# Rotary embedding on one core: float32 instead of bf16, two hardware DMA queues, products split over VectorE and GpSimd

## Chip, core and metric

The kernel runs on one core of a Trainium2 chip. The metric is device time in microseconds (us). The span is the time from the first to the last instruction in the profile; single executions run about 1.7 us above it (170.15 us against 168.4 us before the change). Runs marked slow (over 1.5% above the fastest of the same kernel) are left out of the ratios.

## The reference

x has shape (8, 2048, 8, 64) in float32: batch, position, head, dimension. cos and sin are (2048, 32).

```python
x1, x2 = x[..., :32], x[..., 32:]
out1 = x1 * cos - x2 * sin          # cos, sin broadcast over batch and head
out2 = x1 * sin + x2 * cos
out  = concatenate([out1, out2], axis=-1)
```

x and the output are 33.55 MB each, and the two tables 0.26 MB each. That is 67.6 MB to move for four products and two sums per pair of elements.

## The kernel before

Each of the 128 partitions holds 16 consecutive positions of one batch; a tile is 4 of them, 2048 elements a partition. There are 32 tiles. Everything on chip is bf16. All DMA is issued on GpSimd's queue, and the DMA casts between float32 in DRAM and bf16 in SBUF, the on-chip memory. VectorE does all arithmetic.

```python
for t in range(num_tiles):                       # 32 loads, 20 buffers
    xt = xpool.tile([P, FREE], bf16, tag="xt", name=f"xt{t}")
    nc.gpsimd.dma_start(out=..., in_=xv[b, :, l*SL:(l+1)*SL, :])
...
for t in range(num_tiles):
    eng.tensor_mul(out=t1k, in0=xtv, in1=cb)     # eng is nc.vector
    eng.tensor_mul(out=t2k, in0=xtv, in1=sb)
    eng.tensor_sub(out=otv[:, :, 0:Dh], in0=t1v[:, :, 0:Dh], in1=t2v[:, :, Dh:D])
    eng.tensor_add(out=otv[:, :, Dh:D], in0=t2v[:, :, 0:Dh], in1=t1v[:, :, Dh:D])
    nc.gpsimd.dma_start(out=ov[...], in_=ot...)  # 12 output buffers
```

## Time and profile before

| | before |
|---|---|
| time, median (range) | 170.2 us (169.31 to 170.33), 4 runs |
| span of the profiled run | 168.4 us |
| VectorE busy | 111.7 us, 66% |
| GpSimd busy | 35.3 us, nearly all of it issuing DMA |
| DMA | at nine tenths or more in slices 1 to 37 of 0 to 39 |

The first lines are from the page of the kernel before: busy tenths per slice (40 equal slices of 4.2 us), what the DMA moved per slice, and the HBM totals. DVE is VectorE and POOL is GpSimd.

```profile
DVE  0059999999999950000008999999999999960000
POOL 7512212211221221222122122212212111120000
DMA  3999999999999999999999999999999999999970
GB/s 53 158 209 214 212 214 214 210 215 215 212 214 212 214 212 214 215 213 212 231 414 422 432 426 430 426 428 428 430 426 426 430 428 428 428 426 430 430 267 2
...
HBM read 34.08 MB, written 33.55 MB: 402 GB/s over the span
```

The DMA row is the one without gaps. The step in the GB/s row from about 214 to about 428 is no change of speed. The first half is loads, which are counted as the bf16 bytes they land; each of those bytes is two bytes read. All 67.6 MB at 428 GB/s take 158 us.

Next, groups of instructions: line, engine, operation, output<-inputs, shapes, count | busy us in total, mean ns of one | idle time before them and what ended it.

```profile
L91 DVE TENSOR_TENSOR t<-xt,cos_sb 128x2048 bf16<-128x2048 bf16 x32 | 38.9, 1216 | 10.6 <-DMA xt<-in_x_dram 10.4
...
L98 DVE TENSOR_TENSOR ot<-t,t 128x1024 bf16<-128x1024 bf16 x32 | 21.8, 682 | 27.7 <-DMA out_dram<-ot 27.7
...
L101 POOL DMA_DIRECT2D out_dram<-ot x32 | 17.0, 532 | 65.9 <-DMA out_dram<-ot 29.1 <-DVE ot L99 21.6 <-DMA xt<-in_x_dram 15.2
```

And the waits (who waited for whom: total us, times, longest):

```profile
DVE ot L98 <- DMA out_dram<-ot: 27.7, 1, 27.7
...
DVE t L91 <- DMA xt<-in_x_dram: 10.4, 1, 10.4
```

VectorE waited once for 27.7 us because all output buffers were full and their stores stood behind the loads in one queue. It is an engine with time to spare. The bytes set the time.

### The profile page before, as it was taken

Reading aid. Unit: us, or ns where it says so; the run is one execution under the profiler, and the core shown is the slowest. Engines: PE = TensorE matmul, PEld = TensorE weight load, DVE = VectorE, ACT = ScalarE, POOL = GpSimd, SP = SyncE. Lnnn points to the kernel's source line nnn. Section 1 sums busy time; section 2 is a strip of 40 time slices with the busy share of each in tenths; the row PEclk is TensorE's granted clock in tenths of the full one; section 3 lists DMA queues with packets and bytes.
Section 4 is the critical chain, followed back from the end, with each engine's and each line's share of the span. In section 5 each row is a group of like instructions: output and inputs, shape, how many; then the busy total and the mean of one; then the engine's idle time right before and its main releaser. Section 6 shows DMA issues by size and latency. Waiting matters only on the chain.

```text
span 168.4 us, 282 instructions
## 1 busy us (share of the span) xinstructions
DVE 111.7 (66%) x128; POOL 35.3 (21%) x70
## 2 busy tenths in 40 slices
DVE  0059999999999950000008999999999999960000
POOL 7512212211221221222122122212212111120000
DMA  3999999999999999999999999999999999999970
GB/s 53 158 209 214 212 214 214 210 215 215 212 214 212 214 212 214 215 213 212 231 414 422 432 426 430 426 428 428 430 426 426 430 428 428 428 426 430 430 267 2
DMA packets 9506, 50.61 MB, mean 300 GB/s; under 512 B 1056, under 2 KB 1312, under 8 KB 5408
## 3 DMA queue, kind: packets, MB, share of 16 engines
q0 software_dynamic: 9504, 50.60, 103.5%
q14 instruction: 2, 0.02, 0.0%
HBM read 34.08 MB, written 33.55 MB: 402 GB/s over the span
## 4 chain that ended last, share of the span: by engine, by line
DMA 51%; DVE 24%; issue 12%; POOL 2%; POOLq 0%; DVEq 0%; PEldq 0%
DMA xt<-in_x_dram 39%; DMA out_dram<-ot 12%; DVE t L91 8%; DVE t L92 6%; DVE ot L98 5%; DVE ot L99 5%; POOL out_dram L101 2%; POOL cos_sb L44 0%; POOLq L130 0%; POOL sin_sb L45 0%; POOLq L101 0%; DVEq L98 0%; PEldq L130 0%; POOLq L70 0%
## 5 line engine op out<-in xcount | busy, mean ns | idle before, releaser
L91 DVE TENSOR_TENSOR t<-xt,cos_sb 128x2048 bf16<-128x2048 bf16 x32 | 38.9, 1216 | 10.6 <-DMA xt<-in_x_dram 10.4
L98 DVE TENSOR_TENSOR ot<-t,t 128x1024 bf16<-128x1024 bf16 x32 | 21.8, 682 | 27.7 <-DMA out_dram<-ot 27.7
L92 DVE TENSOR_TENSOR t<-xt,sin_sb 128x2048 bf16<-128x2048 bf16 x32 | 38.9, 1216 | 0.0
L101 POOL DMA_DIRECT2D out_dram<-ot x32 | 17.0, 532 | 65.9 <-DMA out_dram<-ot 29.1
L70 POOL DMA_DIRECT2D xt<-in_x_dram x32 | 16.9, 541 | 48.6 <-DMA xt<-in_x_dram 44.7
L99 DVE TENSOR_TENSOR ot<-t,t 128x1024 bf16<-128x1024 bf16 x32 | 21.8, 681 | 0.0
L44 POOL DMA_DIRECT2D cos_sb<-in_cos_dram x1 | 0.7, 667 | 0.8 <-PEq L130 0.8
L45 POOL DMA_DIRECT2D sin_sb<-in_sin_dram x1 | 0.5, 543 | 0.0
L119 POOL MEMSET const-float32-0.0<- 128x1 f32 x1 | 0.1, 98 | 0.2 <-issue 0.2
L119 POOL MEMSET const-bfloat16-1.0<- 128x1 bf16 x1 | 0.1, 101 | 0.0
L119 POOL MEMSET const-float32-1.0<- 128x1 f32 x1 | 0.1, 98 | 0.0
L119 POOL MEMSET const-uint8-127<- 128x1 uint8 x1 | 0.1, 98 | 0.0
## 6 DMA issues: line engine op xcount, KB each, us to landing
out_dram<-ot POOLq DMA_DIRECT2D x32, 1024.0 KB, 19.1
xt<-in_x_dram POOLq DMA_DIRECT2D x32, 512.0 KB, 19.1
cos_sb<-in_cos_dram POOLq DMA_DIRECT2D x1, 128.0 KB, 3.2
sin_sb<-in_sin_dram POOLq DMA_DIRECT2D x1, 128.0 KB, 3.1
```

The lines of the kernel that those rows point to most:

```text
L44: nc.gpsimd.dma_start(out=cos_sb, in_=cos_src)
L45: nc.gpsimd.dma_start(out=sin_sb, in_=sin_src)
L70: nc.gpsimd.dma_start(out=xt.rearrange("p (r f) -> p r f", r=SL), in_=xv[b, :, l * SL : (l + 1) * SL, :],)
L91: eng.tensor_mul(out=t1k, in0=xtv, in1=cb)
L92: eng.tensor_mul(out=t2k, in0=xtv, in1=sb)
L98: eng.tensor_sub(out=otv[:, :, 0:Dh], in0=t1v[:, :, 0:Dh], in1=t2v[:, :, Dh:D])
L99: eng.tensor_add(out=otv[:, :, Dh:D], in0=t2v[:, :, 0:Dh], in1=t1v[:, :, Dh:D])
L101: nc.gpsimd.dma_start(out=ov[b, :, l * SL : (l + 1) * SL, :], in_=ot.rearrange("p (r f) -> p r f", r=SL),)
L119: nc = _bacc.Bacc("TRN2", target_bir_lowering=False, num_devices=1)
```

## The change

The intent is to compute in float32 throughout without paying for it. The DMA no longer casts, and it moves to the queues of the sync engine (loads) and the scalar engine (stores). GpSimd is then free to do half of the products. Each VectorE product and add in the tile loop reads one operand from PSUM, a second on-chip memory, so that it has only one input in SBUF. The tiles also come in another order (batch innermost). The diff, cut to its core:

```diff
-    nc.gpsimd.dma_start(out=cos_sb, in_=cos_src)          # bf16 tables
-    nc.gpsimd.dma_start(out=sin_sb, in_=sin_src)
+    nc.scalar.dma_start(out=sin_sb, in_=sin_src)          # float32 tables
+    nc.scalar.dma_start(out=cos_sb, in_=cos_src)
...
-        xt = xpool.tile([P, FREE], bf16, ...); nc.gpsimd.dma_start(out=xt..., ...)
+        xt = xpool.tile([P, FREE], f32, ...);  nc.sync.dma_start(out=xt, ...)
...
+    nc.vector.tensor_scalar_mul(ssin[:, :, 0, :], sin_sb, -1.0)   # signed sin
+    nc.vector.tensor_copy(ssin[:, :, 1, :], sin_sb)
+    nc.vector.tensor_copy(cos_ps, cos_sb)                         # cos to PSUM
...
-        eng.tensor_mul(out=t1k, in0=xtv, in1=cb)
-        eng.tensor_mul(out=t2k, in0=xtv, in1=sb)
-        eng.tensor_sub(...); eng.tensor_add(...)
-        nc.gpsimd.dma_start(out=ov[...], in_=ot...)
+        for u in range(2):                                # halves swapped
+            nc.gpsimd.tensor_mul(out=dst..., in0=src..., in1=rep(ssin[..., u, :], H))  # t2, SBUF, 3 buffers
+        nc.vector.tensor_mul(out=t1..., in0=xt..., in1=rep(cos_ps[...], 2 * H))         # t1, PSUM, 1 buffer
+        nc.vector.tensor_add(out=xt, in0=t1, in1=t2)      # in place
+        nc.scalar.dma_start(out=ov[...], in_=xt)
```

More of the change, by code (lines that the diff above doesn't have):

```diff
@@ L20 @@
     f32 = mybir.dt.float32
-    bf16 = mybir.dt.bfloat16
     B, S, H, D = x.shape
@@ L31 @@
     FREE = SL * HD
-    NH = SL * H
-    NK = NH * 2
-    xv = x.rearrange("b (q r) h d -> b q r (h d)", q=P)
-    ov = out.rearrange("b (q r) h d -> b q r (h d)", q=P)
+    xv = x.rearrange("b (q r) h d -> b q (r h d)", q=P)
+    ov = out.rearrange("b (q r) h d -> b q (r h d)", q=P)
     cos_src = cos.rearrange("(q r) d -> q r d", q=P)
@@ L41 @@
     const_pool = ctx.enter_context(tc.tile_pool(name="const", bufs=1))
-    cos_sb = const_pool.tile([P, R, Dh], bf16, tag="cb")
-    sin_sb = const_pool.tile([P, R, Dh], bf16, tag="sb")
-    nc.gpsimd.dma_start(out=cos_sb, in_=cos_src)
-    nc.gpsimd.dma_start(out=sin_sb, in_=sin_src)
-    num_tiles = B * n_blk
-    xpool = ctx.enter_context(tc.tile_pool(name="xpool", bufs=20))
-    tpool = ctx.enter_context(tc.tile_pool(name="tpool", bufs=4))
-    opool = ctx.enter_context(tc.tile_pool(name="opool", bufs=12))
@@ L53, in coef @@
-    def coef(tab, l):
-        a = tab[:, l * SL, :]
-        return dataclasses.replace(
-            a, ap=[a.ap[0][:], [Dh, SL], [0, 2 * H], a.ap[1][:]]
-        )
-    def idx(t):
-        b = t // n_blk
-        l = t % n_blk
-        return b, l
-    eng = nc.vector
-    xts = []
-    for t in range(num_tiles):
-        b, l = idx(t)
-        xt = xpool.tile([P, FREE], bf16, tag="xt", name=f"xt{t}")
-        nc.gpsimd.dma_start(
-            out=xt.rearrange("p (r f) -> p r f", r=SL),
-            in_=xv[b, :, l * SL : (l + 1) * SL, :],
-        )
-        xts.append(xt)
@@ L76 @@
-    for t in range(num_tiles):
-        b, l = idx(t)
-        xt = xts[t]
-        t1 = tpool.tile([P, FREE], bf16, tag="t1")
-        t2 = tpool.tile([P, FREE], bf16, tag="t2")
-        ot = opool.tile([P, FREE], bf16, tag="ot")
-        cb = coef(cos_sb, l)
-        sb = coef(sin_sb, l)
-        xtv = xt.rearrange("p (r k d) -> p r k d", r=SL, d=Dh)
-        t1k = t1.rearrange("p (r k d) -> p r k d", r=SL, d=Dh)
-        t2k = t2.rearrange("p (r k d) -> p r k d", r=SL, d=Dh)
-        eng.tensor_mul(out=t1k, in0=xtv, in1=cb)
-        eng.tensor_mul(out=t2k, in0=xtv, in1=sb)
-        t1v = t1.rearrange("p (h d) -> p h d", d=D)
-        t2v = t2.rearrange("p (h d) -> p h d", d=D)
-        otv = ot.rearrange("p (h d) -> p h d", d=D)
-        eng.tensor_sub(out=otv[:, :, 0:Dh], in0=t1v[:, :, 0:Dh], in1=t2v[:, :, Dh:D])
-        eng.tensor_add(out=otv[:, :, Dh:D], in0=t2v[:, :, 0:Dh], in1=t1v[:, :, Dh:D])
-        nc.gpsimd.dma_start(
-            out=ov[b, :, l * SL : (l + 1) * SL, :],
-            in_=ot.rearrange("p (r f) -> p r f", r=SL),
-        )
+    cps_pool = ctx.enter_context(tc.tile_pool(name="cps", bufs=1, space=bass.MemoryType.PSUM))
@@ new lines @@
+    t1_pool = ctx.enter_context(tc.tile_pool(name="t1p", bufs=1, space=bass.MemoryType.PSUM))
+    xpool = ctx.enter_context(tc.tile_pool(name="xpool", bufs=20))
+    t2_pool = ctx.enter_context(tc.tile_pool(name="t2p", bufs=3))
+    cos_sb = const_pool.tile([P, R, Dh], f32, tag="cb")
+    sin_sb = const_pool.tile([P, R, Dh], f32, tag="sb")
+    ssin = const_pool.tile([P, R, 2, Dh], f32, tag="ss")
+    cos_ps = cps_pool.tile([P, R, Dh], f32, tag="cp")
+    nc.scalar.dma_start(out=sin_sb, in_=sin_src)
@@ new lines, with rep @@
+    nc.scalar.dma_start(out=cos_sb, in_=cos_src)
+    tiles = [(b, l) for l in range(n_blk) for b in range(B)]
+    xts = []
+    for i, (b, l) in enumerate(tiles):
+        xt = xpool.tile([P, FREE], f32, tag="xt", name=f"xt{i}")
+        nc.sync.dma_start(out=xt, in_=xv[b, :, l * FREE : (l + 1) * FREE])
+        xts.append(xt)
+    nc.vector.tensor_scalar_mul(ssin[:, :, 0, :], sin_sb, -1.0)
+    nc.vector.tensor_copy(ssin[:, :, 1, :], sin_sb)
+    nc.vector.tensor_copy(cos_ps, cos_sb)
+    def rep(a, n):
+        return dataclasses.replace(a, ap=[a.ap[0][:], a.ap[1][:], [0, n], a.ap[-1][:]])
@@ new lines @@
+    for i, (b, l) in enumerate(tiles):
+        xt = xts[i]
+        t1 = t1_pool.tile([P, FREE], f32, tag="t1")
+        t2 = t2_pool.tile([P, FREE], f32, tag="t2")
+        for u in range(2):
+            dst = t2.rearrange("p (rh u d) -> p rh u d", u=2, d=Dh)[:, :, u, :]
+            src = xt.rearrange("p (rh u d) -> p rh u d", u=2, d=Dh)[:, :, 1 - u, :]
+            nc.gpsimd.tensor_mul(
+                out=dst.rearrange("p (r h) d -> p r h d", h=H),
+                in0=src.rearrange("p (r h) d -> p r h d", h=H),
+                in1=rep(ssin[:, l * SL : (l + 1) * SL, u, :], H),
+            )
+        nc.vector.tensor_mul(
+            out=t1.rearrange("p (r k d) -> p r k d", r=SL, d=Dh),
+            in0=xt.rearrange("p (r k d) -> p r k d", r=SL, d=Dh),
+            in1=rep(cos_ps[:, l * SL : (l + 1) * SL, :], 2 * H),
+        )
+        nc.vector.tensor_add(out=xt, in0=t1, in1=t2)
+        nc.scalar.dma_start(out=ov[b, :, l * FREE : (l + 1) * FREE], in_=xt)
```

## The prediction

> **What bounds the kernel now.** The DMA engines. In the page's 40 slices DMA is at nine tenths or more from slice 1 to slice 37. The slices before 78 us move about 214 GB/s, those after about 428 GB/s. These are one rate: in the first half the transfers are loads that write bf16, so each byte landed is two bytes read from HBM. Totals agree: 34.08 MB read and 33.55 MB written; 67.6 MB at 428 GB/s is 158 us. Stretch by stretch, DMA starts at about 2.4 us and dies away at 164 us; 4.2 us follow with no transfer. VectorE is 66% busy (bf16 products 1216 ns, half-tile sub and add 682 ns). Its longest waits, in the waits view, are for DMA: 27.7 us once for an output buffer, 10.4 us for the first tile. So VectorE has slack and bytes set the time.
>
> **What the change does.** HBM bytes stay the same: x and out were float32 in DRAM already; only the cast inside the DMA goes. So the roughly 158 us of transfer stays. Removed: 64 issues of 0.53 us on GpSimd, which were not the bound. Added: GpSimd arithmetic. Loads and stores now have separate queues, so they mix instead of running as a load half and a store half.
>
> VectorE: the bf16 records fit (n/2+143) cycles at 0.96 GHz. At one float32 element per cycle a 2048-element op is (2048+143)/0.96 = 2.28 us. Two a tile plus PSUM effects: about 4.6 us, 32 tiles 147 us.
>
> GpSimd: this trace has no arithmetic of it. The Trainium skill, "GPSIMD Engine Reference", section 3.1, gives 4497 ns for a float32 2048-element tensor_tensor (VectorE 2293 ns). Estimate from it: two 1024-element halves take 4.5 to 4.7 us a tile, 32 tiles 147 us. No run here shows it yet.
>
> Contention: the skill's "SBUF — State Buffer", section "Who interferes with whom", says that a VectorE instruction with at most one SBUF input, outside two-port modes, doesn't contend with GpSimd. Here product and add each read one operand from PSUM, so I expect both engines to run at full rate side by side.
>
> **Critical path after.** Two bounds nearly meet.
> Compute: first tile and sin table usable near 7 us, 64 GpSimd ops at 2.33 us start to start end at 156 us, last add 2.3, last store 4.5, end of program 2.2: span 165 us.
> Transfer: start 2 us, 67.6 MB at 415 to 428 GB/s (mixing reads and writes may cost a little) 158 to 163 us, end 4.2: span 164 to 169 us.
> The larger decides; times run 1.7 us above the span (170.15 against 168.4). I predict 168.5 us, 80% range 163.5 to 178. Chances: faster by over 2% 0.28, within 2% 0.45, slower by over 2% 0.27. Doubling VectorE's work per tile costs little as it had slack; the gain is small as the bytes stay.
>
> **What would show each step.**
> - GpSimd: 64 products of about 2.3 us each, 85 to 90% busy from 7 to 156 us.
> - VectorE: 64 ops of about 2.3 us, near 147 us busy; waits short, for t2.
> - DMA slices flat near 415 to 428 GB/s with loads and stores mixed; two queues in place of one; mean near 400 GB/s over the span. No half-rate first half.
> - First VectorE tile op near 6 to 7 us instead of 10.4 us.
> - The chain that ended last alternates GpSimd products and adds, or DMA waits for xt, near the end one store.
>
> **What would make it wrong.** GpSimd slower than estimated with 32-element strided runs: each 0.1 us per op adds 6.4 us. VectorE and GpSimd contending after all: serial, over 200 us. Mixed traffic well under 415 GB/s: 400 would give 177 us. Or mixing faster than 428 GB/s and GpSimd faster than estimated: down to 160 us.

## The result and the profile after

| | before | after |
|---|---|---|
| time, median (range) | 170.2 us (169.31 to 170.33) | 168.09 us (168.06 to 168.34) |
| span of the profiled run | 168.4 us | 166.6 us |
| VectorE busy | 111.7 us | 148.2 us |
| GpSimd busy | 35.3 us (DMA issue) | 146.3 us (products) |

The ratio is 0.9887, with a 95% interval of 0.986 to 0.9914: 1.1% faster, which is "within 2%" in the prediction's terms. Ratios here are the mean time of one kernel's fast runs over that of the other's in the same rounds, so they are not quite the ratio of the medians. The output is correct.

The same lines of the page of the kernel after:

```profile
DVE  0169999999999999999999999999999999999980
POOL 0299999999999999999999999999999999998000
DMA  5999999999999999999999999999999999999656
GB/s 167 424 428 421 374 431 423 433 427 425 431 421 431 429 427 427 425 433 419 433 425 423 433 419 433 423 433 427 425 431 421 431 427 427 429 423 433 285 220 252
...
HBM read 34.08 MB, written 33.55 MB: 406 GB/s over the span
```

The transfer rate is about 427 GB/s from slice 1 to slice 36 (slice 4 apart), and loads and stores now run mixed. The new thing is at the right end: the DMA row falls to 6, 5, 6 while the DVE row still shows 9 and 8. At the end the transfers wait for VectorE, where before VectorE was long done. The groups:

```profile
L73 POOL TENSOR_TENSOR t<-xt,ssin 128x1024 f32<-128x1024 f32 x64 | 146.1, 2341 | 6.8 <-DVE ssin L58 6.8
L78 DVE TENSOR_TENSOR t<-xt,cos_ps 128x2048 f32<-128x2048 f32 x32 | 73.5, 2296 | 1.1
L83 DVE TENSOR_TENSOR xt<-t,t 128x2048 f32<-128x2048 f32 x32 | 73.3, 2291 | 3.3
L60 DVE COPY cos_ps<-cos_sb 128x512 f32<-128x512 f32 x1 | 0.7, 694 | 2.4 <-DMA cos_sb<-in_cos_dram 2.4
```

A VectorE instruction takes 2.29 us for 2048 float32 elements. GpSimd's 64 products fill 146.1 us, which is 2.283 us from start to start; the mean of 2341 ns is larger because records overlap. Now the chain of work that ended last, in order of time (start us, length us, what):

```profile
1.17 8.72 DMA cos_sb<-in_cos_dram
...
9.91 0.70 DVE cos_ps L60
...
10.64 2.31 DVE t L78
...
13.04 2.30 DVE xt L83
...
15.37 2.31 DVE t L78
...
159.52 2.29 DVE xt L83
```

The chain starts with the DMA that brings the cos table: issued at 1.17 us, landed at 9.89. From 10.64 on it is VectorE alone, product and add in turn. The last add starts at 159.52 us and takes 2.29. From the first product to the end of the last add is 151.2 us, or 4.725 us a tile: 4.587 us of work and about 0.14 us between instructions. The page's line puts shares to it:

```profile
DVE t L78 44%; DVE xt L83 44%; DMA cos_sb<-in_cos_dram 5%; DVE cos_ps L60 0%; DVEq L83 0%; ACTq L48 0%
```

Finally stretches of time (start:end, length, busy us of VectorE and GpSimd with counts, clock, DMA share, GB/s):

```profile
160.00:162.00 2.00, 1.81 (x1) 0.00 (x0) 1.00 0.17 70
162.00:164.00 2.00, 0.00 (x0) 0.00 (x0) 1.00 0.73 303
```

Between 160 and 162 us the DMA engines are 17% busy, with the end of the store before the last. Then they have nothing left but the last tile, which VectorE hands over at 161.8 us.

### The profile page after: what moved, and what is told of

The parts are those of the page before. It is cut to its first block, busy times and chain, and to the rows that moved or that the text cites. A ratio compares the mean times of both kernels' runs of the same rounds, so it can differ in the third digit from the quotient of the medians.

```text
span 166.6 us, 381 instructions
## 1 busy us (share of the span) xinstructions
DVE 148.2 (89%) x67; POOL 146.3 (88%) x68
## 3 DMA queue, kind: packets, MB, share of 16 engines
q10 hardware_dynamic: 4896, 34.08, 48.6%
HBM read 34.08 MB, written 33.55 MB: 406 GB/s over the span
## 4 chain that ended last, share of the span: by engine, by line
DVE 89%; DMA 5%; issue 2%; DVEq 0%; ACTq 0%
DVE t L78 44%; DVE xt L83 44%; DMA cos_sb<-in_cos_dram 5%; DVE cos_ps L60 0%; DVEq L83 0%; ACTq L48 0%
## 5 line engine op out<-in xcount | busy, mean ns | idle before, releaser
L73 POOL TENSOR_TENSOR t<-xt,ssin 128x1024 f32<-128x1024 f32 x64 | 146.1, 2341 | 6.8 <-DVE ssin L58 6.8
L83 DVE TENSOR_TENSOR xt<-t,t 128x2048 f32<-128x2048 f32 x32 | 73.3, 2291 | 3.3
L78 DVE TENSOR_TENSOR t<-xt,cos_ps 128x2048 f32<-128x2048 f32 x32 | 73.5, 2296 | 1.1
L60 DVE COPY cos_ps<-cos_sb 128x512 f32<-128x512 f32 x1 | 0.7, 694 | 2.4 <-DMA cos_sb<-in_cos_dram 2.4
```

The costliest lines, as they stand in the source:

```text
L60: nc.vector.tensor_copy(cos_ps, cos_sb)
L73: nc.gpsimd.tensor_mul(out=dst.rearrange("p (r h) d -> p r h d", h=H), in0=src.rearrange("p (r h) d -> p r h d", h=H), in1=rep(ssin[:, l * ...
L78: nc.vector.tensor_mul(out=t1.rearrange("p (r k d) -> p r k d", r=SL, d=Dh), in0=xt.rearrange("p (r k d) -> p r k d", r=SL, d=Dh), in1=rep ...
L83: nc.vector.tensor_add(out=xt, in0=t1, in1=t2)
```

## The experiments

Two theories about the kernel after: **Theory V**: VectorE's chain sets the end; it starts when the cos table lands and runs at 4.725 us a tile, and the transfers alone would be done sooner. **Theory T**: the transfers still set the end, and VectorE only rides along. A rival C blames traffic between GpSimd and VectorE.

### Transfers alone

```diff
-        t1 = ...; t2 = ...; nc.gpsimd.tensor_mul(...) x2; nc.vector.tensor_mul(...); nc.vector.tensor_add(...)
         nc.scalar.dma_start(out=ov[...], in_=xt)
```

> The loads and stores of the changed kernel with no product and no add (wrong result on purpose). Theory V (VectorE's chain, which starts when the cos table lands and runs at 4.725 us a tile, sets the end of the changed kernel): the transfers alone are done sooner, 67.65 MB at 428 GB/s is 158 us, plus about 1.5 us to start and 3 us after the last byte, span 162 to 164 us against 166.6. Theory T (the transfers set the end, VectorE only rides along): span within 0.5 us of 166.6.

Measured: 165.34 us (164.97 to 165.46), span 163.3 us, ratio to before 0.9726 (0.9683 to 0.977). Its output is wrong, which doesn't matter for the time. The row of the page:

```profile
GB/s 169 429 333 429 427 425 427 429 425 429 429 423 429 427 425 429 427 425 427 429 427 425 427 429 425 429 429 423 431 425 425 429 427 425 429 427 427 425 427 249
```

Slice 2 apart, the rate holds at about 427 GB/s to slice 38. So the transfers of the changed kernel need 163.3 us, and it spends 3.3 us more. Theory T falls. The same number also says that the new transfers are 5.1 us shorter than the whole of the kernel before.

### Half of GpSimd's products

```diff
-        for u in range(2):
+        for u in range(1):
...
-        nc.vector.tensor_add(out=xt, in0=t1, in1=t2)
+        nc.vector.tensor_add(out=xt..., in0=t1..., in1=t2b)   # the u = 0 half, read twice
```

> Half of GpSimd's products left out (the add reads the other half twice, same shapes on VectorE; wrong result on purpose). Theory V: GpSimd at 4.57 us a tile was just under VectorE's 4.725, so the time stays within 1 us, and the VectorE records stay at 2296 and 2291 ns because the two don't contend. Rival C (GpSimd's traffic slows VectorE, or the add waits for GpSimd): VectorE's records get shorter or the gap between product and add closes, and the span falls by more than 1.5 us.

Measured: 168.19 us (168.09 to 168.28), span 166.5 us. Its output is wrong, which doesn't matter for the time.

```profile
L73 POOL TENSOR_TENSOR t<-xt,ssin 128x1024 f32<-128x1024 f32 x32 | 74.3, 2324 | 75.2 <-DVE xt L85 68.3 <-DVE ssin L58 6.7 <-DMA xt<-in_x_dram 0.2
...
L85 DVE TENSOR_TENSOR xt<-t,t 128x2048 f32<-128x2048 f32 x32 | 73.3, 2292 | 3.3
```

GpSimd's work fell from 146.1 to 74.3 us, and neither the span (166.6) nor VectorE's record length (2291, now 2292 ns) moved. Rival C falls: GpSimd neither paces nor slows VectorE here.

### Half of VectorE's product

```diff
-            out=t1..., in0=xt..., in1=rep(cos_ps[...], 2 * H))
-        nc.vector.tensor_add(out=xt, in0=t1, in1=t2)
+            out=t1[:, 0:FREE//2]..., in0=xt[:, 0:FREE//2]..., in1=rep(cos_ps[...], H))
+        nc.vector.tensor_add(out=xt..., in0=t1b, in1=t2...)   # half of t1, read twice
```

> VectorE's cos product is done on half the columns (the add reads that half twice; wrong result on purpose): product about 1.23 us, VectorE 3.65 us a tile. Theory V: VectorE no longer sets the pace; GpSimd's 64 products still end near 153.4 us, the last add and store then end near 160.5, so the transfers become the bound and the span falls to 162.5 to 164 us. Theory T: span within 0.5 us of 166.6.

Measured: 165.37 us (165.24 to 165.73), span 163.5 us. Its output is wrong, which doesn't matter for the time. Its waits:

```profile
DVE xt L85 <- POOL t L73: 31.5, 31, 1.3
```

The span lands on the floor that the transfers alone gave (163.3). VectorE now waits for GpSimd before 31 of 32 adds, so GpSimd paces the arithmetic, but at 4.57 us a tile it ends early enough to stay hidden. With this run, both sides of theory V are shown: less work on VectorE brings the time to the floor, less on GpSimd does nothing.

### Tables at the head of the load queue

```diff
-    nc.scalar.dma_start(out=sin_sb, in_=sin_src)
-    nc.scalar.dma_start(out=cos_sb, in_=cos_src)
+    nc.sync.dma_start(out=sin_sb, in_=sin_src)
+    nc.sync.dma_start(out=cos_sb, in_=cos_src)
```

> Both tables go to the head of the sync queue, ahead of x. Theory V: the tables land near 5 us instead of 6.7 and 9.9, the first product starts when the first tile lands (about 7 us instead of 10.6), the first add then waits for GpSimd's first two products and starts near 11.5 us instead of 13.04, so the span falls by about 1.5 us, to about 165.1. Theory T: the same bytes in another order, span unchanged within 0.5 us.

The profiled run fits: span 165.2 us, 1.4 less, with the first product at 6.97 us and the first add at 11.63. But over six runs the median was 169.38 us (167.16 to 169.96, the slowest marked slow), ratio 0.996 (0.9911 to 1.0008). The kernel as a whole did not get faster, and three runs not marked slow took 169.3 to 169.5 us, more than any run of the changed kernel. Two more runs were made to catch a slower one in a trace.

> The tables-first version again, for a trace of one of its slower runs (four of its six took 169.3 to 170.0 us, the traced one 167.2). If the spread comes from loads that arrive later than they are used in some runs, a slower run shows GpSimd or VectorE waiting for x in mid-run; if from the end, the last stores land later. A run near 167.2 again tells nothing of it.

> The same again, a second chance for a trace of a slower run; expectations as for the run before it.

They took 170.15 and 169.58 us (single runs, state unknown), so both are of the slower kind. None of the expected causes was right: nothing waits in mid-run, and the last store takes no longer. These are the first waits of GpSimd, of the fast run and then of the two slower ones:

```profile
POOL t L73 <- DMA xt<-in_x_dram: 6.6, 1, 6.6
```

```profile
POOL t L73 <- DMA xt<-in_x_dram: 9.6, 1, 9.6
```

```profile
POOL t L73 <- DMA xt<-in_x_dram: 8.9, 1, 8.9
```

The first tile of x lands 3.0 and 2.3 us later than in the fast run, and the spans are 3.0 and 2.3 us longer (168.2 and 167.5 against 165.2). The chain is shifted as a whole, because nothing later in it has slack. The transfers themselves were slow in those microseconds. The same stretch from 4 to 6 us in the fast run and in the slowest:

```profile
4.00:6.00 2.00, 0.88 (x2) 0.00 (x0) 1.00 0.98 410
```

```profile
4.00:6.00 2.00, 0.81 (x2) 0.00 (x0) 1.00 0.87 258
```

Why the rate there is 258 GB/s in one execution and 410 in another stays open. What follows is that the start of the chain is worth its full length one for one, and that this order of loads makes it uncertain.

### The changed kernel again, and two versions of its ends

Three kernels ran together on one chip. The first is the changed kernel, unedited:

> The changed kernel once more, unedited, beside the next ones on the same chip and with more rounds. Both theories: span 166.3 to 166.6 us, time near 168.1, with a spread of a few tenths. If it shows values up to 170, as the tables-first version did in most of its runs, then the spread belongs to the design and not to the order of the tables.

Measured: 167.93 us (167.87 to 168.43), span 166.3 us, ratio 0.9895 (0.9871 to 0.992). The tables' spread does not belong to the changed kernel as such.

The second cuts only the last tile into pieces of 2, 1 and 1 positions:

```diff
+    LAST = (2, 1, 1)          # rows of the last tile; each piece has its own load, products, add and store
```

> Only the last tile is cut into pieces of 2, 1 and 1 rows. VectorE pays about 0.9 us more of fixed cost (its chain ends near 162.7 instead of 161.8), but the last store is 256 KB instead of 1 MB and lands about 2.1 us after its issue instead of 3.9. Theory V: span about 165.7, 0.9 us less. Theory T: unchanged.

Measured: 167.37 us (167.3 to 167.49), span 165.7 us, ratio 0.9857 (0.9834 to 0.988). The span is as expected. Beside the changed kernel of the same rounds the saving is 0.56 us (167.93 to 167.37); 0.9 was expected, from an earlier trace of 166.6 us.

The third also puts the tables first and cuts the first tile:

```diff
+    FIRST, LAST = (1, 1, 2), (2, 1, 1)
-    nc.scalar.dma_start(out=sin_sb ...); nc.scalar.dma_start(out=cos_sb ...)
+    nc.sync.dma_start(out=sin_sb ...);   nc.sync.dma_start(out=cos_sb ...)
```

> Tables at the head of the sync queue, first tile cut into 1, 1 and 2 rows, last into 2, 1 and 1. Theory V: the first add starts near 7 us instead of 13.04, the VectorE chain ends near 159.5 us and the last small store lands near 162, so the transfers' floor (163.3 us of span when they ran alone) is the bound: span 163.3 to 164.5, time 165.2 to 166.5. If the tables' place on the sync queue is what spread the times of the tables-first version, this one spreads likewise, up to 3 us.

Measured: 166.63 us (166.33 to 167.54), span 164.6 us, ratio 0.9827 (0.9794 to 0.9859); the result is correct. It is the fastest correct kernel, 1.7% faster than before (the interval leaves open whether it is over 2%), and it is 1.3 us above the transfers' floor in span. Its times spread over 1.2 us, less than the 2.8 (2.3 without the run marked slow) of the version with the tables alone moved. The step that missed: the first add started at 8.12 us and not near 7, and VectorE's chain ended at 161.4 us and not at 159.5. The waits show why:

```profile
DVE xt L96 <- POOL t L86: 2.1, 3, 1.0
```

Three adds of the first two tiles wait for GpSimd's products, 2.1 us in all (0.78, 0.30 and 1.00). In the same profiled run the stretch from 4 to 6 us moved only 246 GB/s, as slow as in the slow run above, and the time was still among the shortest: the first piece of 256 KB had landed by 6.6 us.

### Nothing in PSUM

```diff
-    cps_pool = ...tile_pool(name="cps", bufs=1, space=PSUM)
-    t1_pool  = ...tile_pool(name="t1p", bufs=1, space=PSUM)
+    cps_pool = ...tile_pool(name="cps", bufs=1)      # SBUF
+    t1_pool  = ...tile_pool(name="t1p", bufs=1)      # SBUF
```

> The cos table and t1 live in SBUF instead of PSUM, so each VectorE product and add has two SBUF inputs; the result is right. Theory V with the contention that the PSUM placement avoids: VectorE ops wait for GpSimd's 2.3 us products or the other way about; in the extreme the two engines take turns, 4.6 + 4.6 us a tile, 32 tiles 294 us, and the time is 200 to 310 us. Rival (no contention in 1x float32 ops): within 2 us of 168.

Measured: 291.56 us (291.39 to 291.65), ratio 1.7169 (1.712 to 1.7219); the result is correct.

```profile
L73 POOL TENSOR_TENSOR t<-xt,ssin 128x1024 f32<-128x1024 f32 x64 | 271.2, 4272 | 6.7 <-DVE ssin L58 6.7
L78 DVE TENSOR_TENSOR t<-xt,cos_ps 128x2048 f32<-128x2048 f32 x32 | 135.4, 4230 | 1.1
L83 DVE TENSOR_TENSOR xt<-t,t 128x2048 f32<-128x2048 f32 x32 | 133.2, 4164 | 3.3
```

All three groups nearly double in length, for the same elements. It is not that SBUF operands are slow in themselves. GpSimd's last product ends at 278.25 us, and the last two VectorE instructions, which run without it, are back at full speed with both inputs in SBUF:

```profile
280.43 2.29 DVE L78 TENSOR_TENSOR t<-xt,cos_ps 128x2048 f32<-128x2048 f32 x1
282.83 2.29 DVE L83 TENSOR_TENSOR xt<-t,t 128x2048 f32<-128x2048 f32 x1
```

While both work, a tile takes 8.66 us (the products of two successive tiles start at 98.67 and 107.33 us), close to the sum of the two engines' lone times, 4.587 + 4.566 = 9.15 us. For most of the time the engines take turns. The Trainium skill says why, in "SBUF — State Buffer", section "Who interferes with whom": a VectorE instruction with two SBUF inputs contends with a GpSimd instruction that reads SBUF, and one with a single SBUF input, outside VectorE's two-port modes, does not. Both halves of that agree: 2291 and 2296 ns with the PSUM operand, 4164 and 4230 ns without.

### All DMA issued on GpSimd

```diff
-        nc.sync.dma_start(...)    nc.scalar.dma_start(...)
+        nc.gpsimd.dma_start(...)  nc.gpsimd.dma_start(...)
```

> The changed kernel with all its loads and stores issued on GpSimd's queue, as before the change. GpSimd's 64 products take 146 us and 64 issues of about 0.53 us another 34, and a store's issue, which must wait for VectorE's add, holds up the products behind it: at least 7 + 180 + 8 = 195 us, up to 330 if each tile's product, add and store run one after the other. Rival (issue cost is hidden): about 168 us.

Measured: 259.5 us (one run), span 257.7 us; the result is correct.

```profile
DVE xt L83 <- POOL t L73: 91.2, 25, 30.8
POOL xt L55 <- DMA out_dram<-xt: 27.9, 7, 7.9
```

The loads and stores now stand among the products in GpSimd's one stream of instructions. Where a load has to wait for a buffer that a store must free, the products behind it wait too (one load waited 7.6 us, until 81.95, and the next product started at 84.94), and VectorE waits for them: 91.2 us in all. In this program, moving the DMA off GpSimd is thus what makes it usable for arithmetic; another order of issue on GpSimd was not tried.

This trace also shows the two ends of a queue on GpSimd with plain float32 transfers. In the first 10 us it moves 2.2 MB, where the changed kernel moves 3.2 (the rates of its stretches times their lengths). After its last data, at about 253.6 us, 4.1 us pass to the end of the span; with the transfers alone on the hardware queues it was 1.7 us (data end near 161.6, span 163.3).

### Less work on VectorE, in the kernel before

```diff
-        eng.tensor_mul(out=t2k, in0=xtv, in1=sb)
-        t2v = t2.rearrange(...)
+        t2v = t1.rearrange(...)
```

> The kernel before with its second product left out (sub and add read t1 twice; wrong result on purpose): VectorE's work falls from 111.7 to about 73 us, the transfers stay. If the transfers bind the kernel before, as the prediction read it: time within 1% of before. Rival (VectorE's stretches without waits in the second half, 90 to 131 us, cost something): faster by over 2 us.

Measured: 170.02 us (169.72 to 170.52), span 168.4 us, ratio 1.0031 (0.9948 to 1.0113). Its output is wrong, which doesn't matter for the time.

```profile
DVE 77.6 (46%) x96; POOL 35.3 (21%) x70
```

VectorE's busy time fell from 111.7 to 77.6 us and the time did not follow. The kernel before is bound by its transfers.

## Why the prediction was right or wrong

The measured 168.09 us lies 0.4 us from the predicted 168.5, and "within 2%" was the likeliest of the three forecasts. Some of its steps were still wrong, and two errors cancelled: the transfers' bound was put too high and the compute bound too low. That the number came so close is in part luck.

- **What bounds the kernel before: the transfers.** Right, and shown by the last experiment. The bytes did stay the same (34.08 MB read, 33.55 MB written in both).
- **"Mixing reads and writes may cost a little", 415 to 428 GB/s.** The top of the range: the mixed stretches hold 427 GB/s. The flat 358 GB/s that "SBUF — State Buffer" advises for such estimates (section "Summary: rules for kernel authors") would have given 189 us; this trace disagrees with it. "HBM Reference" (section "Specifications") explains the gap: 358 is the share with both cores of a pair streaming, and one core alone reached about 425 GB/s; the 427 here agrees.
- **The transfer bound, "span 164 to 169 us".** Too high: 163.3. The step that failed is its last term, "end 4.2", which was copied from the kernel before. On the hardware queues it measured 1.7 us. The gain that the prediction did not see is here: the same bytes start sooner (in the first 10 us the kernel before read about 2.4 MB, at 120 GB/s of landed bf16, and the transfers alone moved 3.0) and finish with less behind them. That it is the queue and not the cast is supported, though not isolated, by the run with all DMA on GpSimd, whose float32 transfers had the slow start and a 4.1 us ending.
- **VectorE about 4.6 us a tile.** The work is 4.587 us, and the rate behind the estimate holds: 1024 float32 elements took 1.228 us in the run with half a product and 2048 took 2.296, which is 1.04 ns an element, twice the 0.52 ns of bf16 (1216 less 682 ns for 1024 elements). But the period is 4.725. VectorE idles about 0.10 us before each add, which reads the product's result, and 0.03 us before each product (3.3 and 1.1 us in the groups above): 0.14 us a tile, 4.4 us over 32 tiles. The estimate had no term for that; no run tries to shorten it.
- **GpSimd at 4.5 to 4.7 us a tile.** Right: 4.566. The figure of the "GPSIMD Engine Reference", section 3.1, 4497 ns for 2048 elements, is 1.5% below this trace's two 1024-element halves, for runs of 32 elements with a repeated operand.
- **No contention thanks to PSUM.** Right, and worth 123 us.
- **The compute bound, 165 us.** It measured 166.6. The prediction let GpSimd pace it and start near 7 us. GpSimd did start at 7.25, but the critical engine was VectorE, which could not start before the cos table, at 10.64 us. In the terms of the sum: 7 + 149 to the end of GpSimd's work and 9.0 after it were forecast; 10.6 to VectorE's start, 151.2 of its chain and 4.8 after it were measured, so the ending, put too long, hid part of the error. "First VectorE tile op near 6 to 7 us" failed, and so did the forecast of the chain. The sin table (6.0 us to land) and the cos table (8.7 us) took that long beside the first tiles of x; ahead of them in the load queue, or in GpSimd's (3.0 and 3.1 us with all DMA there), each took about 3 us. The "DMA: Bandwidth & Descriptors" page, section "Queues, rings and completion order", says that each DMA engine takes turns between its queues packet by packet; the late tables agree with that, though no run here varies the packets.
- **"The larger decides."** Right as a rule, wrong as to which. The prediction saw the transfers as the likely larger bound; measured, it was compute by 3.3 us.
- **"Doubling VectorE's work per tile costs little as it had slack."** Loosely put, since busy time rose by a third (111.7 to 148.2 us), and it did not come free: VectorE's chain, with its late start, costs the 3.3 us above the floor.

So the expected "little change" was a gain and a loss: 5.1 us won on the transfers (168.4 to 163.3), 3.3 us given back to VectorE's chain, 1.8 us left. These are spans of the profiled runs; by the medians of the same rounds (170.08 and 165.34 us) the transfers won 4.7 us.

## What to carry to other kernels

When a change takes the kernel from one bound to another that is nearly as high, compute each bound with its own start and its own end, and run the transfers alone to know the floor; here a forecast of the total was right with the wrong engine on the chain. Bring small tables that the first instruction needs ahead of large loads, but measure several executions, because the order of the first loads also changed the spread. Here GpSimd did half of the products, a third of the element operations, beside VectorE at full rate, with one operand of each VectorE instruction in PSUM and no DMA issued on GpSimd.

## What the Trainium skill lacked or had wrong

- "SBUF — State Buffer", Summary: it advises about 358 GB/s for transfers between HBM and SBUF without the condition that "HBM Reference" gives, both cores of a pair streaming. One core alone moved 427 GB/s here, loads and stores mixed; no page gives a figure for the mix.
- "SBUF — State Buffer", Who interferes with whom: right about who contends. A lock held for the whole of each instruction would give, as an estimate from the lone times, 9.15 us a tile; the run without PSUM took 8.66, so about 0.5 us of a tile's four instructions lies outside the turns.
- "DMA: Bandwidth & Descriptors": no figure for a small load beside large ones on another queue. Tables of 256 KB landed 6.0 and 8.7 us after their issue there, and 2.8 and 2.9 us at the head of the load queue.
- No page says how the end of a program depends on the queue: 1.7 us from last data to the end with the hardware queues (those of the sync and scalar engines), 4.1 us with the software queue (GpSimd's).
- No page has the spread of the first load: with the tables first, the first tile of x was usable at 6.97 us in one execution and at 9.99 us in another.
- "GPSIMD Engine Reference", section 3.1: only one length, 2048 elements, with no word on their layout; here 1024 elements in runs of 32 with a repeated operand took 2.283 us from start to start.
